# Second norm's weight and bias applied in the second feed-forward's input stage, via DRAM; last norm's as fused VectorE operations

## The chip, the cores and the metric

The kernel runs on one core of a Trainium2 chip. The metric is the device time of one execution in microseconds. The engines are TensorE (PE, matmuls), VectorE (DVE), ScalarE (ACT), GpSimd (POOL) and SyncE (SP), which issues most of the DMAs. Each engine works through its own instructions in a fixed order and waits for the others on semaphores.

## The reference

One layer of an encoder on 1024 tokens of 1024 features in float32, in three sub-layers with a residual and a norm each. The change touches the second norm and the third sub-layer:

```
h  = x * (1 + scale) + shift                    # modulation, from the vector c
y  = (silu(h @ w_in[:, :2816]) * (h @ w_in[:, 2816:])) @ w_out
x  = layer_norm(ALPHA * x + 0.5 * (1 + gate) * y) * g + b
```

The mixer before it ends in the same way, with ln2_g and ln2_b. The third sub-layer uses the mixer's normed result twice: in h, and in the residual ALPHA * x. The output is the third sub-layer's x, with ln3_g and ln3_b.

## The kernel before, in words

All products are done as three float32r products of a high and a low part: `split` has ACT write the high part (L139, a cast) and DVE the low part (L140, a tensor_tensor). The tile names end in h and l, or the halves of one tile are the two parts (gl, wr).

The second feed-forward has two stages. The input stage, `in_phase`, goes through 22 steps j; a step is a pair of column tiles of w_in, whose seven Strassen-Winograd products PE makes (L378). The weights of step j + 1 are loaded and prepared during step j: `in_load` loads them into the tiles "ra" and "rb", two buffers each, on SP (L340); `in_gate` and `in_sums` make the operands "ah", "al", "sh", "sl" (L355 to L358 are the sums on DVE). The results go to DRAM tiles gd (L399). After each step from 2 on a hook is called; in the second feed-forward, `hook2` computes the gate row gate2 at steps 10 to 15, from loads of w_ada (L162) through heap slots. The heap has 30 slots of 4 KB per partition; the right operands of the stage take 28.

The output stage, `out_phase`, multiplies what lies in gd by w_out, in seven products numbered 2, 1, 3, 6, 5, 7, 4, each over 11 steps, four token tiles and three matmuls (L589). `prep` loads gd and w_out four steps ahead (L556, L549) and splits them; at products 1, 5 and 6 DVE also makes sums of the weights (L570, L571, L581, L583). When a product ends, its four PSUM banks are read (L608 to L632), times the gate row (L599), and added to ALPHA * x (L596). `xs2` brings x: the mixer's normed rows before weight and bias, which `done2` stored in the DRAM tiles spill2 (L1257). It loads a row tile (L1417) and has POOL multiply by ln2_g (L266) and add ln2_b (L267), both 128x1024, in `affine`. The rows of weight and bias are loaded into SBUF once, as a broadcast to all partitions (L262).

`done3` is the last norm of a tile. Tiles 0 to 3 are finished after product 5, between the steps of product 7; tiles 4 to 7 after product 4, the last, in which the tiles' matmuls end one after the other. For tiles 0 to 6 `norm_tile` makes the statistics (L247, L249), the reciprocal root in ten small steps (L213 to L223), a factor nm (L256), and has ACT scale (L257); then POOL applies ln3_g and ln3_b to each half (L266, L267), and SP stores it (L1432). Tile 7 takes another way: DVE subtracts the mean and multiplies by ln3_g in one operation of 1024 columns (L1437), multiplies by the reciprocal root and adds ln3_b in one for each half (L1440), and SP and ACT store one half each.

Each engine's order is made ahead of time by a planner from estimated durations and the place in the program; instructions whose inputs the planner expects early are drawn ahead of their place. Buffers with one tag are handed out in turn, and a tile's load waits until the last reader of the buffer's former tile is done.

The first feed-forward uses the same `in_phase` and `out_phase`. There x comes from the input without weight and bias, and its norm is scaled on ACT alone.

Of the kernel before, what the change touches and what calls it, by code (L numbers as in the profile page):

```python
# [7 lines left out]
F32 = mybir.dt.float32  # L8
# [7 lines left out]
P = 128  # L16
# [34 lines left out]
def layer_kernel(ctx, tc, a, out):  # L51
# [26 lines left out]

# [1 line left out]
    c_raw = const.tile([P, KD], F32, name="c_raw")  # L80
# [61 lines left out]

# [1 line left out]
    w_ada = a["w_ada"][0].rearrange("(p j) n -> p j n", j=KD)  # L144
# [64 lines left out]

# [1 line left out]
    def rstd_of(var, eps, name):  # L211
# [56 lines left out]

# [1 line left out]
    def transpose4(name, srcs):  # L270
# [7 lines left out]

    # Strassen-Winograd right operands of a pair of feature tiles (2 k, 2 k + 1); token halves are the columns.
    def right_first(name, ops, hb, eng=V):  # L280
        """hb: feature tiles 2 k and 2 k + 1 of token half 0."""
        hi, lo = slot(f"{name}bh"), slot(f"{name}bl")
        split(hi, lo, hb, eng)
        ops["B11"].append((hi[:, 0], lo[:, 0]))
        ops["B21"].append((hi[:, 1], lo[:, 1]))

    def right_second(name, ops, hb, hc, eng=G, lo=V):
        """hc: feature tiles 2 k and 2 k + 1 of token half 1."""
        t12 = slot(f"{name}t12", dt=F32)
        eng.tensor_tensor(t12[:, 0], hc[:, 0], hb[:, 0], ALU.subtract)  # L290
        eng.tensor_tensor(t12[:, 1], hc[:, 1], t12[:, 0], ALU.subtract)
        right_t(name, ops, 1, t12, lo)
        return t12
# [23 lines left out]

# [1 line left out]
    TAGS = {  # L319
# [4 lines left out]
    def in_tags(wp, order):  # L324
        """Has the tiles that are free first lie first."""
        for tag in order.split():
            shape, bufs = TAGS[tag]
            wp.tile(shape, F32, tag=tag, bufs=bufs, name=f"{tag}_")
# [43 lines left out]
    def product(ps, left, right, ks=range(4), more=False):  # L372
        """more: on top of the sum that the bank holds."""
        wh, wl = left
# [17 lines left out]
    def in_steps(wp, s, j, L, ops, gd, begun={}):  # L392
        """The seven products of a pair of gate and up tiles; the left operands of the second half to DRAM."""
        q = G if j >= NJ - 1 else SY
# [10 lines left out]
        def prod(left, right, ps=None):  # L405
            """ps: the bank that holds the sum so far."""
            if left in begun:
                return begun[left]
            more = ps is not None
            ps = ps if more else bank(f"fi{s}_{j}{left}")  # L410
            product(ps, L[left], ops[right], more=more)
            return ps
# [120 lines left out]

    # ---- SwiGLU, second half: product with w_out in Strassen-Winograd form (token halves, halves of the columns,
    # even and odd feature tiles), residual; done(t) follows each finished token tile; after(half, k) the tiles
    # of a half, some way into the next products ----
    def out_phase(s, wp, w_out, gd, gate, xs, done, after, hook):
# [13 lines left out]
        def prep(n, k):  # L551
            """Operands of step k of product n; wa holds B11, then T1, and B22, wb B12, then T3, and B21, then T4."""
            if (n, k) in left:
# [137 lines left out]

    # ================= sub-layer 1 =================
    x_in = a["x"][0]
    with pool("p1a") as wp:
# [27 lines left out]
        def first_mod(kk, raws, n):  # L722
            """The last n of its four blocks are summed on the vector engine first."""
            ps = wide(f"ada0p{kk}")
# [46 lines left out]
        def early(wp, s, w_in, ops):  # L771
# [9 lines left out]

            # a: ada loads, x: token loads, w: weights, M: modulation, H: modulated features, R: right
            # operands, G and S: left operands, g: products; "d" has the vector engine take more of it
            for tok in SEQ.split():
# [49 lines left out]
    rows = tc.alloc_tile_pool(name="rows", bufs=1, reuse_waits="tile", side="right")  # L834
    gate1 = rows.tile([P, D], F32, name="gate1")
    mix_in = a["mix_w_in"][0]
# [59 lines left out]

    # ================= sub-layer 2 =================
    mxb = tc.alloc_tile_pool(name="mxb", bufs=1, reuse_waits="tile", side="right")
# [191 lines left out]
    with pool("mattn") as wp:  # L1090
# [64 lines left out]

        # LayerNorm over the channels of the convolution, in place, between the steps of the attention
        cstat = {}
# [78 lines left out]

    spill2 = [dram.tile([P, D], F32, name=f"spill2_{t}", tag="spill2", bufs=NT) for t in range(NT)]
    ops = new_ops()
    hb, hc = [None] * 4, [None] * 4
    todo2 = {}  # L1240
    TENG = (V, G)
    with pool("p3a") as wp:
# [59 lines left out]
        def play(st, tokens):  # L1302
            """m: output projection, d: residual norm, f and F: features of the token halves, r: B11 and B21,
            b: B22, s, t: sums and parts of T1 and T2, u, v: of T3 and T4, G: A11, A12 and A22, X, x: sums and
            parts of S1 and S2, Y, y: of S3 and S4, p: products, W: the next weights; a capital letter at the
            end is the engine, "!" keeps the order on the engine."""
            n3 = {t[-2]: t[-1] for t in reversed(tokens) if t.lstrip("!")[0] == "p" and t[-1] in "35"}
# [77 lines left out]
        play(None, first)  # L1385

        def hook2(j):
            if j in (10, 13):
                if j == 10:
                    mods["gate2"] = slot("gate2", (P, D), F32)  # L1390
                todo2[j + 2] = ada_gate(wp, raw_slot, 2, 0.5, mods["gate2"], (j - 10) // 3)
            if j in todo2:
                todo2.pop(j)()
# [9 lines left out]
    raw_pool[2].release()  # L1403
    rows.release()

    with pool("p3b") as wp:
        xt2 = {}
        got2 = set()
        rows2 = []
        fin = []  # L1410

        def xs2(t):
            if t not in got2:
                got2.add(t)
                if t not in xt2:
                    xt2[t] = wp.tile([P, D], F32, tag="x", bufs=XB, name=f"x2_{t}")
                SY.dma_start(xt2[t], spill2[t])  # L1417
                if not rows2:
                    rows2.extend((row_bcast("ln2_g", wp), row_bcast("ln2_b", wp)))
                affine(xt2[t], *rows2)  # L1420
            return xt2[t]

        def done3(t):
            if not fin:
                fin.extend((row_bcast("ln3_g"), row_bcast("ln3_b")))
            rows_ = out[t * P : (t + 1) * P, :]
            if t < NT - 1:
                norm_tile(xt2[t], f"3_{t}")
                for h in range(2):
                    hs = slice(h * H, (h + 1) * H)  # L1430
                    affine(xt2[t][:, hs], fin[0][:, hs], fin[1][:, hs])
                    SY.dma_start(rows_[:, hs], xt2[t][:, hs])  # L1432
                return
            x = xt2[t]
# [7 lines left out]

        out_phase(2, wp, a["ffn2_w_out"][0], gd, mods["gate2"], xs2, done3, lambda half, k: None, lambda gi, j: None)


# [35 lines left out]
```

## Time and profile before

| | us |
|---|---|
| three runs | 1960.56, 1960.99, 1962.79 |
| median | 1960.99 |
| profiled execution, first to last instruction (span) | 1958.3 |
| PE busy | 1832.7 (94%) |
| DVE busy | 1538.3 (79%) |
| ACT busy | 781.3 (40%) |
| POOL busy | 405.6 (21%) |

The profiled execution's own time is taken as its span and what lies around it. The page cuts the span into 40 slices of 49 us; a digit is a busy share in tenths, PEclk the clock granted to TensorE in tenths of full speed:

```profile
PE   5899999999999999999999859989999999997896
DVE  8867768675697978999689989896565756589888
POOL 2200000000000020168476561430000000036034
PEclk7899999999999999999999879989999999998998
```

The second feed-forward's input stage fills slices 27 to 34, its output stage the last five. Busy times of PE are from modelled ends; a matmul of 512 columns is shown with 0.39 us and the next one starts earlier.

### The profile page before, as it was taken

Reading aid. Unit: us, or ns where it says so; the run is one execution under the profiler, and the core shown is the slowest. Engines: PE = TensorE matmul, PEld = TensorE weight load, DVE = VectorE, ACT = ScalarE, POOL = GpSimd, SP = SyncE. Lnnn points to the kernel's source line nnn. Section 1 sums busy time; section 2 is a strip of 40 time slices with the busy share of each in tenths; the row PEclk is TensorE's granted clock in tenths of the full one; section 3 lists DMA queues with packets and bytes.
Section 4 is the critical chain, followed back from the end, with each engine's and each line's share of the span. In section 5 each row is a group of like instructions: output and inputs, shape, how many; then the busy total and the mean of one; then the engine's idle time right before and its main releaser. Section 6 shows DMA issues by size and latency. Waiting matters only on the chain. (4 is left out here: it accounts for less than half of the span.)

```text
span 1958.3 us, 23453 instructions
## 1 busy us (share of the span) xinstructions
PE 1832.7 (94%) x8562; PEld 1514.4 (77%) x8562; DVE 1538.3 (79%) x2276; ACT 781.3 (40%) x1240; POOL 405.6 (21%) x280
## 2 busy tenths in 40 slices
PE   5899999999999999999999859989999999997896
PEld 4688888888888788888888748768888888885675
DVE  8867768675697978999689989896565756589888
ACT  3423333333445441142677642643333333443541
POOL 2200000000000020168476561430000000036034
PEclk7899999999999999999999879989999999998998
DMA  8527445533885322110000032234333432574511
GB/s 251 166 92 223 157 140 188 167 119 130 302 282 155 113 95 62 33 44 33 1 1 1 25 124 78 97 114 139 102 100 116 129 97 86 192 261 155 162 65 70
DMA packets 201394, 238.39 MB, mean 122 GB/s; under 512 B 13866, under 2 KB 124575, under 8 KB 201278
## 3 DMA queue, kind: packets, MB, share of 16 engines
q1 hardware_dynamic: 197786, 225.06, 35.7%
q0 software_dynamic: 2112, 7.34, 1.0%
q10 hardware_dynamic: 1380, 4.49, 0.6%
q8 instruction: 67, 1.10, 0.2%
q14 instruction: 49, 0.40, 0.1%
HBM read 183.89 MB, written 52.95 MB: 121 GB/s over the span
## 5 line engine op out<-in xcount | busy, mean ns | idle before, releaser
L589 PE MATMUL fo<-wr,gl 128*128 128x512 f32 x1848 | 430.4, 394 | 25.8 <-DVE wr L140 13.3
L589 PEld LDWEIGHTS fo<-wr,gl 128*128 128x128 f32 x1848 | 349.2, 190 | 105.0 <-DVE wr L140 16.0
L140 DVE TENSOR_TENSOR sl<-sf,sh 128x1024 fp32r<-128x1024 f32 x87 | 110.6, 1272 | 145.2 <-ACT sh L139 145.2
L139 ACT CAST sh<-sf 128x1024 fp32r<-128x1024 f32 x88 | 92.7, 1053 | 209.9 <-issue 31.5
L399 POOL DMA_DIRECT2D gd<-gf x8 | 4.5, 568 | 824.9 <-DVE gf L465 824.3
L932 DVE SCALAR_TENSOR_TENSOR cacc<-u,convw,cacc 128x1015 f32<-128x1015 f32 (+14 forms) x120 | 152.3, 1319 | 0.9
L140 DVE TENSOR_TENSOR gl<-gr,gl 128x512 fp32r<-128x512 f32 x148 | 110.6, 754 | 8.1 <-ACT gl L139 6.7
L139 ACT CAST gl<-gr 128x512 fp32r<-128x512 f32 x148 | 90.6, 618 | 64.1 <-DMA gr<-gd 56.2
L153 DVE SCALAR_TENSOR_TENSOR ada<-adaw,c_act,ada 128x512 f32<-128x512 f32 x98 | 73.3, 748 | 36.5 <-DMA adaw<-in_w_ada_dram 35.7
L266 POOL TENSOR_TENSOR x<-x,row_ln_g 128x1024 f32<-128x1024 f32 (+1 forms) x28 | 65.0, 2334 | 169.1 <-ACT x L257 100.8
L1058 DVE TENSOR_REDUCE mx<-sc 128x1 f32<-128x1024 f32 x64 | 76.1, 1216 | 19.8 <-PE sc L1056 19.8
L1060 ACT ACTIVATE p<-sc,mx 128x1024 f32<-128x1024 f32 x64 | 71.3, 1115 | 48.0 <-DVE mx L1058 46.7
L139 ACT CAST ah<-ra 128x1536 fp32r<-128x1536 f32 x44 | 65.0, 1478 | 58.6 <-DMA ra<-in_ffn_w_in_dram 14.4
L140 DVE TENSOR_TENSOR al<-ra,ah 128x1536 fp32r<-128x1536 f32 x44 | 77.1, 1751 | 1.2 <-ACT ah L139 1.2
L427 ACT ACTIVATE gf<-gf 128x512 f32<-128x512 f32 x44 | 27.8, 632 | 118.5 <-DVE gf L426 109.7
L140 DVE TENSOR_TENSOR wr<-wa,wr 128x512 fp32r<-128x512 f32 x66 | 54.1, 819 | 23.7 <-ACT wr L139 23.6
L1293 PE MATMUL mo<-moh,fh 128*128 128x512 f32 x128 | 51.3, 401 | 20.7 <-DVE x L1297 20.1
L139 ACT CAST wr<-wa 128x512 fp32r<-128x512 f32 x66 | 41.1, 622 | 62.4 <-PE fo L589 61.8
L913 PE MATMUL glu<-hm,gluh 128*128 128x512 f32 x256 | 65.7, 392 | 0.0
L1112 POOL TENSOR_TENSOR p<-p,p 128x1024 f32<-128x1024 f32 x27 | 64.8, 2401 | 1.9
L1129 PE MATMUL av<-vf,aT 128*128 128x128 f32 x512 | 62.7, 276 | 1.2 <-ACT cacc L1190 0.8
L139 ACT CAST wr<-wb 128x512 fp32r<-128x512 f32 x66 | 40.1, 620 | 55.3 <-PE fo L589 45.3
(3503 smaller groups left out, 4858.8 us busy)
## 6 DMA issues: line engine op xcount, KB each, us to landing
gr<-gd SPq DMA_DIRECT2D x148, 256.0 KB, 3.0
ra<-in_ffn_w_in_dram SPq DMA_DIRECT2D x132, 256.0 KB, 4.1
adaw<-in_w_ada_dram SPq DMA_DIRECT2D x56, 512.0 KB, 4.0
gd<-gf SPq DMA_DIRECT2D x102, 256.0 KB, 2.1
rb<-in_ffn_w_in_dram SPq DMA_DIRECT2D x44, 256.0 KB, 3.1
wb<-in_ffn_w_out_dram SPq DMA_DIRECT2D x44, 256.0 KB, 5.0
wa<-in_ffn_w_out_dram SPq DMA_DIRECT2D x44, 256.0 KB, 4.8
gd<-s SPq DMA_DIRECT2D x40, 256.0 KB, 4.2
```

The costliest lines, as they stand in the source:

```text
L139: a = S.copy(hi, x)
L140: b = eng.tensor_tensor(lo, x, hi.bitcast(F32), ALU.subtract)
L153: V.scalar_tensor_tensor(acc, raw[:, jj], c_act[:, n : n + 1], acc, ALU.mult, ALU.add)
L266: eng.tensor_tensor(x, x, g, ALU.mult)
L589: PE.matmul(ps, lhsT=g[:, x, ts_], rhs=w[:, y], start=n in (1, 2, 3) and k == i == 0, stop=k == NK - 1 and i == 2, skip_group_check=n not ...
L913: PE.matmul(q[2 * m + h], lhsT=w[:, m * P : (m + 1) * P], rhs=hm[k][h][:, x], start=k == 0 and n == 0, stop=k == KD - 1 and n == 2,)
L932: V.scalar_tensor_tensor(acc[:, lo_t:hi_t], u[:, lo_t + sh : hi_t + sh], convw[:, i, jj : jj + 1], acc[:, lo_t:hi_t], ALU.mult, ALU.add,)
L1058: V.tensor_reduce(mx_, ps, axis=AX.X, op=ALU.max, negate=True)
L1060: S.activation(pe, ps, AF.Exp, bias=mx_, accum_out=sm[:, e : e + 1])
L1112: last = G.tensor_tensor(p0, p0, p1, ALU.add)
L1129: PE.matmul(ps[:, 0:P], lhsT=aT[:, kt], rhs=vf[kt][:, h * P : (h + 1) * P], start=kt == 0, stop=kt == 7)
L1293: pe = PE.matmul(ps, lhsT=x[:, ts_], rhs=w[:, ds_], start=n == 0, stop=n == total - 1)
```

## The change

The second norm's weight and bias are applied earlier, and the result goes through DRAM once more. In steps 2 to 9 of the second feed-forward's input stage, `hook2` calls `residual_tile`: it loads a row tile of spill2 on SP into a buffer of the tag "ra" (shared with the weight tiles of `in_load`), has DVE multiply by ln2_g and add ln2_b, and stores it on SP into new DRAM tiles spill3. The two rows ln2_g and ln2_b take heap slots from step 2 to step 9. `xs2` then loads from spill3, and POOL does nothing there. gate2 lies where gate1 lay (the pool rows, released later), and not in a heap slot. `done3` treats tiles 0 to 6 as tile 7 was treated: one fused DVE operation of 1024 columns and two of 512, and one store from SP and one from ACT.

```diff
     rows = tc.alloc_tile_pool(name="rows", bufs=1, reuse_waits="tile", side="right")
-    gate1 = rows.tile([P, D], F32, name="gate1")
+    gate1 = rows.tile([P, D], F32, tag="gate1", name="gate1")
...
+        rows2 = []
+
+        def residual_tile(t):
+            if t == 0:
+                rows2.extend((row_bcast("ln2_g"), row_bcast("ln2_b")))
+            x = raw_pool[2].tile([P, 3, 4, P], F32, tag="ra", bufs=2, name=f"x2a_{t}")
+            x = x.rearrange("p a b c -> p (a b c)")[:, 0:D]
+            SY.dma_start(x, spill2[t])
+            affine(x, *rows2, V)
+            SY.dma_start(spill3[t], x)
+            if t == NT - 1:
+                rows2.clear()
+
         def hook2(j):
+            if j < NT + 2:
+                residual_tile(j - 2)
             if j in (10, 13):
                 if j == 10:
-                    mods["gate2"] = slot("gate2", (P, D), F32)
+                    mods["gate2"] = rows.tile([P, D], F32, tag="gate1", name="gate2")
...
-                SY.dma_start(xt2[t], spill2[t])
-                if not rows2:
-                    rows2.extend((row_bcast("ln2_g", wp), row_bcast("ln2_b", wp)))
-                affine(xt2[t], *rows2)
+                SY.dma_start(xt2[t], spill3[t])
             return xt2[t]
...
         def done3(t):
             if not fin:
                 fin.extend((row_bcast("ln3_g"), row_bcast("ln3_b")))
             rows_ = out[t * P : (t + 1) * P, :]
-            if t < NT - 1:
-                norm_tile(xt2[t], f"3_{t}")
-                for h in range(2):
-                    hs = slice(h * H, (h + 1) * H)
-                    affine(xt2[t][:, hs], fin[0][:, hs], fin[1][:, hs])
-                    SY.dma_start(rows_[:, hs], xt2[t][:, hs])
-                return
             x = xt2[t]
             mv = tile_stats(x, f"3_{t}")
             r = rstd_of(mv[:, 1:2], EPS, f"3_{t}")
             V.scalar_tensor_tensor(x, x, mv[:, 0:1], fin[0], ALU.subtract, ALU.mult)
             for h in range(2):
                 hs = slice(h * H, (h + 1) * H)
                 V.scalar_tensor_tensor(x[:, hs], x[:, hs], r, fin[1][:, hs], ALU.mult, ALU.add)
                 (SY, S)[h].dma_start(rows_[:, hs], x[:, hs])
```

## Rows read from the trace of the kernel before

**Rows 1.** Windows: stretch, length, busy us (instructions) by engine, granted clock, DMA share, GB/s.
```profile
1775.00:1800.00 25.00, 12.82 (x39) 9.38 (x38) 25.00 (x18) 4.03 (x7) 17.68 (x7) 0.74 0.40 127
1800.00:1850.00 50.00, 41.29 (x172) 32.99 (x171) 45.48 (x68) 26.34 (x48) 11.19 (x2) 0.93 0.43 129
```
**Rows 2.** Windows of equal length in the first and the second output stage.
```profile
490.50:699.00 208.50, 208.43 (x920) 170.50 (x920) 178.15 (x324) 100.81 (x171) 7.87 (x11) 1.00 0.61 203
1701.40:1909.90 208.50, 182.75 (x774) 148.12 (x774) 185.66 (x267) 92.04 (x156) 71.38 (x31) 0.95 0.51 174
```
**Rows 3.** PE's groups, first and second output stage; then a wait in the second.
```profile
L589 PE MATMUL fo<-wr,gl 128*128 128x512 f32 x924 | 212.8, 391 | 0.1
...
L589 PE MATMUL fo<-wr,gl 128*128 128x512 f32 x924 | 217.5, 397 | 25.8 <-DVE wr L140 13.3 <-ACT pu L608 7.6 <-DVE pv L632 4.9
...
ACT gl L139 <- DMA gr<-gd: 51.0, 22, 9.8
```
**Rows 4.** Timeline of PE: start, length, what, how many in the row.
```profile
1500.73 0.39 PE L378 MATMUL fi_11A<-r_0t3h,ah 128*128 128x512 f32 x1
...
1503.45 0.39 PE L378 MATMUL fi_12A<-r_0bh,ah 128*128 128x512 f32 x1
...
1696.70 9.68 PE L589 MATMUL fo<-wr,gl 128*128 128x512 f32 x42
...
1909.47 30.54 PE L589 MATMUL fo<-wr,gl 128*128 128x512 f32 x132 [1.70 <-DVE pv L632]
```
**Rows 5.** Timeline of POOL in the second output stage.
```profile
1741.78 2.67 POOL L266 TENSOR_TENSOR x<-x,row_ln_g 128x1024 f32<-128x1024 f32 x1 [40.02 <-DMA row_ln_g<-in_ln_g_dram]
...
1810.54 2.72 POOL L267 TENSOR_TENSOR x<-x,row_ln_b 128x1024 f32<-128x1024 f32 x1
```
**Rows 6.** Timeline of DVE at that time.
```profile
1742.10 2.90 DVE L571 TENSOR_TENSOR wb<-wb,t 128x512 f32<-128x512 f32 x1
...
1758.97 0.68 DVE L571 TENSOR_TENSOR wb<-wb,t 128x512 f32<-128x512 f32 x1
```
**Rows 7.** Timeline of DVE in the last four tiles.
```profile
1925.76 0.69 DVE L599 TENSOR_TENSOR ev<-fo,gate 128x512 f32<-128x512 f32 x1 [1.64 <-PE fo L589]
...
1927.21 1.29 DVE L247 BATCH_NORM_STATS2 st<-x 128x6 f32<-128x512 f32 x2
...
1930.53 0.16 DVE L221 SCALAR_TENSOR_TENSOR rz<-rt,rz 128x1 f32<-128x1 f32 x1
1930.72 0.15 DVE L223 TENSOR_SCALAR rr<-rz 128x1 f32<-128x1 f32 x1
1930.79 0.68 DVE L599 TENSOR_TENSOR ev<-fo,gate 128x512 f32<-128x512 f32 x1
...
1945.40 0.68 DVE L599 TENSOR_TENSOR ev<-fo,gate 128x512 f32<-128x512 f32 x1
...
1947.89 2.01 DVE L1437 SCALAR_TENSOR_TENSOR x<-x,mv,row_ln_g 128x1024 f32<-128x1024 f32 x1
...
1952.60 0.87 DVE L221 SCALAR_TENSOR_TENSOR rz<-rt,rz 128x1 f32<-128x1 f32 x1
...
1953.69 1.42 DVE L1440 SCALAR_TENSOR_TENSOR x<-x,rr,row_ln_b 128x512 f32<-128x512 f32 x2
```
**Rows 8.** Timeline of DVE, then of SP, around one weight tile of the input stage.
```profile
1351.27 0.69 DVE L355 TENSOR_TENSOR sf<-rb,ra 128x512 f32<-128x512 f32 x1
...
1368.57 1.23 DVE L140 TENSOR_TENSOR sl<-sf,sh 128x1024 fp32r<-128x1024 f32 x1 [0.22 <-ACT sh L139]
...
1372.12 1.75 DVE L140 TENSOR_TENSOR al<-ra,ah 128x1536 fp32r<-128x1536 f32 x1
...
1373.90 1.47 SPq L340 DMA_DIRECT2D ra<-in_ffn_w_in_dram  x3
```
**Rows 9.** Windows: one step of the input stage.
```profile
1351.40:1370.40 19.00, 19.00 (x85) 15.73 (x84) 12.16 (x17) 6.36 (x9) 0.00 (x0) 1.00 0.41 139
```
**Rows 10.** DMA issues: KB each, median us from issue to landing.
```profile
ra<-in_ffn_w_in_dram SPq DMA_DIRECT2D x132, 256.0 KB, 4.1
```

More of the change, by code (lines that the diff above doesn't have):

```diff
@@ L1237, in layer_kernel @@
     spill2 = [dram.tile([P, D], F32, name=f"spill2_{t}", tag="spill2", bufs=NT) for t in range(NT)]
+    spill3 = [dram.tile([P, D], F32, name=f"spill3_{t}", tag="spill3", bufs=NT) for t in range(NT)]
     ops = new_ops()
@@ L1403, in layer_kernel @@
     raw_pool[2].release()
-    rows.release()
     with pool("p3b") as wp:
@@ L1408, in layer_kernel @@
         got2 = set()
-        rows2 = []
         fin = []
@@ L1443, in layer_kernel @@
         out_phase(2, wp, a["ffn2_w_out"][0], gd, mods["gate2"], xs2, done3, lambda half, k: None, lambda gi, j: None)
+    rows.release()
 _INS = [
```

## The prediction

> **What bounds the kernel now.** The page comes first: TensorE (PE) is busy for 94% of the span and VectorE (DVE) for 79%, and the slices of the page's second part put most of the missing 6% of PE at the beginning, once in the middle, and in the last fifth. [...]
>
> This is the second feed-forward's product with w_out. Its twin, the same function for the first feed-forward, is the best control there is: in 208.5 us of it PE is busy for 208.4, although DVE is busy for 178 [rows 2]. In an equal stretch of the second one PE has 182.8. The groups of PE's instructions name who is late: the 924 matmuls of the phase have 0.1 us of idle time before them in the twin and 25.8 here, 13.3 for DVE's low parts of the weights, 7.6 for an ACT copy and 4.9 for the sums on pv [rows 3].
>
> What does the second have and the first not? POOL. In the second, POOL multiplies by ln2_g and adds ln2_b, sixteen operations, the first and the last in [rows 5]. Just there a 128x512 tensor_tensor of DVE takes 2.90 us, and 0.68 us as soon as POOL rests [rows 6]; six in a row are that long. POOL and DVE stand in each other's way, so some 40 us of POOL work, which nobody seems to wait for, is what makes DVE late.
>
> The size of the loss: PE's first matmul of the phase starts at 1696.70 us, the last run of them ends at 1909.47 + 30.54 = 1940.01 [rows 4], 243.3 us. That the 924 matmuls are 7 products x 11 steps x 4 tiles x 3 stands in the code; twelve take 1503.45 - 1500.73 = 2.72 us at the full clock [rows 4], so 0.2267 us each and 209.5 us in all. The loss is 33.8 us: 25.8 of waiting and 8.0 that the lower clock after the waits costs. Behind PE stands a tail of 1958.3 - 1940.0 = 18.3 us, in which DVE is hardly ever idle.
>
> **The change part by part.** The profiled execution's span is 1958.3 us; the median of the runs is 1960.99, so 2.7 us lie around it, and they stay.
>
> (a) The sixteen POOL operations leave the phase, and the two row loads with them. With POOL silent DVE does as in the twin, and PE needs 209.5 us: -33.8. Bounds: 0 if POOL were not the cause, -33.8 at best, since nothing below 209.5 can be had. I take the whole, because the twin loses 0.1 us with the same products, the same buffers but two and the same DVE work [rows 2].
>
> (b) In the first seven tiles of the last norm, nm on DVE, the scaling on ACT and four POOL operations become one DVE operation of 1024 columns and two of 512. At 1024 columns DVE takes 1.23 us for two inputs from SBUF [rows 8]; the pair of 512 took 1.42 [rows 7]; 2.6 us a tile. Tiles 0 to 3 fall into product 7, where DVE must read pv in time or PE can't begin product 4. That is 10.6 us more DVE work, against the POOL work that disturbs it there now. The wait is 4.9 us now [rows 3]; the twin, which in the same product sums 8 blocks for a gate, has none. Bounds 0 and 4.9 + 2.8, the latter because ACT now issues the second store of each tile and holds the casts queued behind it until DVE's last half (0.7 us, four tiles). I take 1.0, near the twin.
>
> (c) The tail. DVE's last four tiles begin at 1925.76 and end at 1953.69 + 1.42 = 1955.11, 29.35 us [rows 7]. PE's last four groups, of 7 steps x 3 matmuls, end 21 x 0.2267 = 4.8 us apart and are faster than that: DVE sets the end. Tile 4 takes 1930.79 - 1925.76 = 5.0 us undisturbed. Tile 7 takes 1955.11 - 1945.40 = 9.7 and has the fused form already, but its 1024-wide operation takes 2.01 instead of 1.23, and three of the one-column L221 steps are stretched, at 0.87 against 0.16 in the worst: together 2.6 us, so 7.1 undisturbed. The other three have one more 0.6 us of statistics (two took 1.29): 3 x 7.7 + 7.1 = 30.2. So +0.9. What the disturbance gives back the fused work takes. Bounds +0.9 and -2.7: a step that needs the one before it starts 0.19 us later (1930.53 to 1930.72), a step of another tile 0.07 later (1930.72 to 1930.79) [rows 7], and three chains of ten such steps between another tile's operations would save up to 3.6. I take +0.9, since today's order hardly mixes the tiles. [...]
>
> (d) In the input stage DVE gets sixteen 128x1024 operations at 1.23 us, 19.7 us, two to a step from step 2 to 9. A step lasts 19 us, and DVE works 12.2 of them in the fuller kind [rows 9], so 2.5 us fit into 6.8 idle ones. Bounds: 0 (PE has no gap here to gain) and 19.7 if every one delays PE. I take 1.0 for the whole stage: an operation that stands in DVE's order before its 512 KB have landed holds the reads of PSUM behind it, and PE's next product into that bank waits for those.
>
> (e) SP gets eight loads, eight stores and two row loads there, each issue under 0.5 us, and each store holds SP until DVE has added the bias; behind it stand the next weights and the gd stores. The cover is that a weight tile is issued a step ahead. But the loaded row tile takes one of the two "ra" buffers in turn with the weights, so that these are single-buffered for eight steps. Now: DVE first reads a weight tile at 1351.27, last at 1372.12 + 1.75 = 1373.87, and the load into that buffer is issued at 1373.90 [rows 8] and lands 4.1 us after issue, three in a row: some 5.6 us [rows 10]. With one buffer this tile's load would start when the tile before it was read, a step earlier, at 1354.8, and end by 1360.4. What its sums feed is needed by DVE at 1368.57 [rows 8], and two sums of 0.7 us and a cast of ACT of about 1 us come before that: some 5 us are to spare. Cost 0; without that cover see the second rival.
>
> (f) gate2 leaves the heap for the place of gate1. Its two rounds of loads and sums lose their free heap slots to the two rows and come later than now, into the same idle DVE time; it is needed at the start of the phase some 200 us on. 0.
>
> Sum: -33.8 + 1.0 + 0.9 + 1.0 = -30.9; span 1927.4, with the 2.7 us around it **1930 us**.
>
> **The rivals.**
> *Loads, not DVE, set products 6 and 5.* The 7.6 us wait for the ACT copy came when DVE had caught up, and ACT's casts stood behind loads of gr, 51.0 us in all [rows 3]. If it stays with its share of the slow clock (some 2.4) and product 7's wait grows to the 7.7 of (b), the time is 1930 + 10 + 6.7 = 1947. For: the fused work comes in the same products. Against: the twin moves 203 GB/s where this one moves 174 [rows 2], without a wait.
> *Slower: the single weight buffer decides.* If DVE's first read keeps its place in the order, a tile's cycle is 22.6 us of reading and 5.6 of loading, 28.2 against 19.04 a step: +9.2 us in each of eight steps, 73 in all, 2003 us. It decides from 30.9 / 8 = 3.9 us a step on. For: the sums are read early today. Against: they are read early because nothing holds them, and 5 us are to spare.
> *The added DVE work is exposed.* 18.7 more than I took in (d): 1949 us. Against: 6.8 idle us a step.
> *POOL is not the cause, and the moved work changes nothing:* 1961. The stretch from 0.68 to 2.90 us in step with POOL speaks against it.
>
> **How the numbers follow.** Forecast 0.68, loads and product 7 0.13, exposed DVE work 0.08, single buffer 0.08, no change 0.03. The forecast's own range goes from 1924.6 (no losses in (b) and (d), the tail at -2.7) to 1938, with the small terms at several times my value. With the first rival it reaches 1947 and holds four in five: 1924 to 1947. Under 0.2%, some 4 us, a measurement of this kernel tells nothing from no change: faster 0.89, same 0.03, slower 0.08.
>
> **What would show it.** After: no POOL operation but the gate's copy in the phase; no 128x512 operation of DVE over 1 us; PE's phase at 210 to 212 us from first to last matmul with a clock of 1.0 (a); no wait of PE for DVE's wr (a), under 2 us for pv (b); 29 to 30 us from the first ev of the tail to DVE's end (c); steps of 19.0 us in the input stage while the row tiles pass (d, e). Steps of 20 us or more there, or PE waiting for ah or sh, would make the prediction wrong, and so would a wait for the ACT copy of pu that stays.

## The result and the profile after

The changed kernel takes 1924.64 us (median of 1924.09, 1924.61, 1924.68 and 1927.3) against 1961.14 us of the kernel before on the same chip: a ratio of 0.9821, 95% interval 0.9807 to 0.9834. The prediction of 1930 us had the direction and the place; 5.4 us of the gain of 36.5 were not forecast, and the result lies at the lower end of the forecast's own range (1924.6 to 1938). The profiled run of the changed kernel is the slowest of the four, with a span of 1925.5 us.

First the windows that answer to [rows 1]; the columns are the same.

```profile
1775.00:1800.00 25.00, 25.00 (x112) 20.71 (x111) 24.67 (x40) 12.64 (x23) 0.00 (x0) 1.00 0.34 103
1800.00:1850.00 50.00, 50.00 (x221) 41.15 (x220) 33.14 (x52) 29.44 (x51) 0.00 (x0) 1.00 0.51 161
```

PE (first) works without a gap at the full clock (1.00). DVE (third) does 40 operations in the first window where it did 18, in the same busy time, and in the second it rests for 16.9 us. POOL (fifth) is silent.

PE's group of the output stage, and its timeline, answer to the second row of [rows 3] and the last of [rows 4]:

```profile
L589 PE MATMUL fo<-wr,gl 128*128 128x512 f32 x924 | 210.2, 389 | 0.1
```
```profile
1700.65 210.31 PE L589 MATMUL fo<-wr,gl 128*128 128x512 f32 x924
```

All 924 products stand in one row, since nothing waits: 210.3 us where it was 243.3. The waits for wr, pu and pv are gone.

DVE in the first 19 us of what was POOL's stretch (1741 to 1760), by groups: count, busy us, mean ns of one. [rows 6] had 2.90 us there.

```profile
L140 DVE TENSOR_TENSOR gl<-gr,gl 128x512 fp32r<-128x512 f32 x8 | 5.5, 684 | 0.0
L583 DVE TENSOR_TENSOR wb<-wa,wb 128x512 f32<-128x512 f32 x8 | 5.4, 684 | 0.0
```

The tail answers to [rows 7]. These are the first and last rows of DVE there, the `ev` of each tile, and at the second tile a few small steps beside it.

```profile
1897.39 0.69 DVE L599 TENSOR_TENSOR ev<-fo,gate 128x512 f32<-128x512 f32 x1 [0.28 <-PE fo L589]
1898.12 0.69 DVE L596 SCALAR_TENSOR_TENSOR x<-x,ev 128x512 f32<-128x512 f32 x1
1898.85 1.29 DVE L247 BATCH_NORM_STATS2 st<-x 128x6 f32<-128x512 f32 x2
...
1900.35 1.27 DVE L1442 SCALAR_TENSOR_TENSOR x<-x,mv,row_ln_g 128x1024 f32<-128x1024 f32 x1
1901.54 0.15 DVE L216 TENSOR_SCALAR rz<-rv 128x1 int32<-128x1 int32 x1
1901.60 0.68 DVE L599 TENSOR_TENSOR ev<-fo,gate 128x512 f32<-128x512 f32 x1
1902.20 0.14 DVE L217 TENSOR_SCALAR rz<-rz 128x1 int32<-128x1 int32 x1
...
1906.29 0.68 DVE L599 TENSOR_TENSOR ev<-fo,gate 128x512 f32<-128x512 f32 x1
...
1912.27 0.68 DVE L599 TENSOR_TENSOR ev<-fo,gate 128x512 f32<-128x512 f32 x1
...
1920.95 1.42 DVE L1445 SCALAR_TENSOR_TENSOR x<-x,rr,row_ln_b 128x512 f32<-128x512 f32 x2
```

From the first `ev` to DVE's end it is 1922.37 - 1897.39 = 25.0 us, 29.4 before. Tile 5's `ev` (1901.60) stands between two steps of tile 4's square root (L216 and L217): the work of two tiles is mixed. In the kernel before, tile 4's small steps run to the last one, L223 at 1930.72, ahead of tile 5's `ev` at 1930.79 [rows 7], and one small operation of tile 4 (nm) stands behind it:

```profile
1931.39 0.21 DVE L256 TENSOR_SCALAR nm<-mv,rr 128x1 f32<-128x1 f32 x1
```

The input stage grew. DVE's two operations on the row tiles, with what ended the idle time before them, then one of the two steps where PE lost time (step 8; step 9 follows):

```profile
L266 DVE TENSOR_TENSOR x2a<-x2a,row_ln_g 128x1024 f32<-128x1024 f32 x8 | 9.8, 1223 | 10.7 <-DMA x2a<-spill 9.1 <-DMA gd<-gf 1.7
L267 DVE TENSOR_TENSOR x2a<-x2a,row_ln_b 128x1024 f32<-128x1024 f32 x8 | 9.8, 1223 | 0.2
```
```profile
1440.11 1.23 DVE L266 TENSOR_TENSOR x2a<-x2a,row_ln_g 128x1024 f32<-128x1024 f32 x1 [1.61 <-DMA x2a<-spill]
...
1444.89 0.49 DVE L151 TENSOR_SCALAR ada<-adaw,c_act 128x512 f32<-128x512 f32 x1 [1.17 <-DMA adaw<-in_w_ada_dram]
1445.30 0.68 DVE L357 TENSOR_TENSOR sf<-ra,rb 128x512 f32<-128x512 f32 x1
1445.90 0.68 DVE L443 TENSOR_TENSOR p<-fi_8A,p 128x512 f32<-128x512 f32 x1
...
1462.27 1.54 DVE L153 SCALAR_TENSOR_TENSOR ada<-adaw,c_act,ada 128x512 f32<-128x512 f32 x2 [2.72 <-DMA adaw<-in_w_ada_dram]
```
```profile
1446.63 0.50 PE L378 MATMUL fi_8A<-r_0t3h,ah 128*128 128x512 f32 x1 [0.52 <-DVE p L443]
```

In step 8 DVE waits for a load of the row tile, then for one of the gate's columns (adaw), and the sum on `p`, which frees PE's bank, stands behind both. In step 9 it stands behind the gate's columns alone (2.72 us). From the start of its first product to that of the next step's, step 8 lasts 19.90 us and step 9 20.25, where steps 4 to 7, and the same two in the kernel before, last 19.04. The gate's first sum is at 1444.89 us here; it was at 1307.44 in the kernel before and is at 1306.82 in the run without the residual tiles ("No detour" below), so the tiles and their two rows push the gate's loads back into steps 8 and 9. From the first product of the input stage to the first of the output stage it is 1700.65 - 1257.12 = 443.5 us, 441.8 before. This is one run; the second profile of the same kernel (below) has 442.9.

The span in four stretches, both profiled runs, each end taken from PE's timeline:

| stretch | before | after | difference |
|---|---|---|---|
| start to first product of the second input stage | 1254.9 | 1257.1 | +2.2 |
| input stage | 441.8 | 443.5 | +1.8 |
| output stage, PE | 243.3 | 210.3 | -33.0 |
| end of PE to the end | 18.3 | 14.6 | -3.7 |
| span | 1958.3 | 1925.5 | -32.8 |

The same code runs in the first row's stretch. The ten profiled runs that have the residual tiles began their input stage at 1254.8 to 1261.0 us (1257.0 on the mean), the four that have not at 1254.3 to 1256.5 (1255.2). These ranges overlap; whether the change has a part in the 2.2 us is not shown.

### The profile page after: what moved, and what is told of

Same layout as the page of the kernel before. It is cut to its first block, busy times and chain, and to the rows that moved or that the text cites. A ratio compares the mean times of both kernels' runs of the same rounds, so it can differ in the third digit from the quotient of the medians.

```text
span 1925.5 us, 23435 instructions
## 1 busy us (share of the span) xinstructions
PE 1829.6 (95%) x8562; PEld 1512.7 (79%) x8562; DVE 1518.1 (79%) x2306; ACT 773.0 (40%) x1233; POOL 321.0 (17%) x236
## 4 chain that ended last, share of the span: by engine, by line
PE 70%; DVE 16%; issue 8%; DMA 3%; ACT 2%; POOL 1%; SPq 1%; DVEq 0%; POOLq 0%; ACTq 0%
PE fo L589 19%; PE mo L1294 4%; PE vp L961 2%; DVE mx L1058 2%; PE qp L961 2%; PE fi_16A L378 1%; PE fi_15A L378 1%; PE fi_10A L378 1%; PE fi_6A L378 1%; PE fi_2A L378 1%; PE fi_21A L378 1%; PE fi_19A L378 1%; PE fi_20A L378 1%; PE fi_18A L378 1%; PE fi_17A L378 1%
## 5 line engine op out<-in xcount | busy, mean ns | idle before, releaser
L589 PE MATMUL fo<-wr,gl 128*128 128x512 f32 x1848 | 423.1, 390 | 0.2
L140 DVE TENSOR_TENSOR sl<-sf,sh 128x1024 fp32r<-128x1024 f32 x87 | 109.4, 1259 | 116.0 <-ACT sh L139 115.8
L140 DVE TENSOR_TENSOR gl<-gr,gl 128x512 fp32r<-128x512 f32 x148 | 102.1, 696 | 6.9 <-ACT gl L139 5.5
L140 DVE TENSOR_TENSOR al<-ra,ah 128x1536 fp32r<-128x1536 f32 x44 | 77.0, 1750 | 1.3 <-ACT ah L139 1.2
L427 ACT ACTIVATE gf<-gf 128x512 f32<-128x512 f32 x44 | 27.8, 632 | 124.1 <-DVE gf L426 113.7
L140 DVE TENSOR_TENSOR wr<-wa,wr 128x512 fp32r<-128x512 f32 x66 | 45.5, 689 | 27.4 <-ACT wr L139 27.2
L1129 PEld LDWEIGHTS av<-vf,aT 128*128 128x128 f32 x512 | 60.9, 195 | 1.7 <-ACT cacc L1190 1.0
```

The costliest lines, as they stand in the source:

```text
L140: b = eng.tensor_tensor(lo, x, hi.bitcast(F32), ALU.subtract)
L589: PE.matmul(ps, lhsT=g[:, x, ts_], rhs=w[:, y], start=n in (1, 2, 3) and k == i == 0, stop=k == NK - 1 and i == 2, skip_group_check=n not ...
L1129: PE.matmul(ps[:, 0:P], lhsT=aT[:, kt], rhs=vf[kt][:, h * P : (h + 1) * P], start=kt == 0, stop=kt == 7)
```

## The experiments

The theory: VectorE is held up by GpSimd when both work on whole tiles, and this alone makes PE wait. The rivals: the loads, the dependences of the residual, or the order of VectorE's work.

| kernel | median us | ratio to before, 95% | input stage | PE in output stage | behind PE |
|---|---|---|---|---|---|
| part one alone | 1935.05 | 0.9859 (0.9841 to 0.9877) | 441.3 | 215.5 | 18.2 |
| part two alone | 1951.44 | 0.9950 (0.9935 to 0.9964) | 440.9 | 238.7 | 14.6 |
| GpSimd beside, two inputs | 1952.85 | 0.9953 (0.9939 to 0.9968) | 441.5 | 237.4 | 14.6 |
| GpSimd beside, one input | 1943.94 | 0.9919 (0.9903 to 0.9936) | 441.1 | 229.4 | 14.6 |
| GpSimd beside, fills | 1925.39 | 0.9817 (0.9802 to 0.9833) | 441.9 | 210.3 | 14.8 |
| no detour | 1923.28 | 0.9807 (0.9793 to 0.9822) | 441.1 | 210.3 | 15.1 |
| VectorE in the output stage | 1925.27 | 0.9823 (0.9809 to 0.9838) | 440.7 | 210.3 | 15.3 |
| tail in turn | 1928.33 | 0.9836 (0.9821 to 0.9850) | 442.1 | 210.3 | 19.4 |
| nine steps apart | 1925.24 | 0.9821 (0.9806 to 0.9835) | 441.4 | 210.3 | 14.1 |
| ScalarE's statistics | 1925.19 | 0.9820 (0.9806 to 0.9834) | 442.7 | 210.9 | 15.3 |
| the same, nine steps apart | 1923.85 | 0.9816 (0.9802 to 0.9830) | 441.1 | 211.1 | 13.6 |
| the changed kernel again | 1923.07 | 0.9813 (0.9799 to 0.9827) | 442.9 | 210.3 | 14.6 |

The last three columns are us of each profiled run, worked out as in the table above. Each ratio is to the kernel before in runs beside it, whose medians were 1959.6 to 1962.0 us. Line numbers in the rows of an experiment are those of its own kernel: where an edit adds lines, L599 can become L601 or L602, and L596 become L599.

**Part one alone, and part two alone.** The first restores the old branch of `done3`, the second is the kernel before without that branch.

```diff
             rows_ = out[t * P : (t + 1) * P, :]
+            if t < NT - 1:
+                norm_tile(xt2[t], f"3_{t}")
+                for h in range(2):
+                    hs = slice(h * H, (h + 1) * H)
+                    affine(xt2[t][:, hs], fin[0][:, hs], fin[1][:, hs])
+                    SY.dma_start(rows_[:, hs], xt2[t][:, hs])
+                return
```

> The changed kernel with the second part undone: token tiles 0 to 6 are normed and then multiplied and added in halves on GpSimd again, the residual stays as changed. Theory (GpSimd beside VectorE in the output stage makes VectorE slow, each part carries its own price): the loss beside the first eight residual tiles is gone, but the wait of the products on the operands in the last product (4.9 us before) and the 29.4 us of the last four tiles come back, so the time is 1924.6 + about 9 = 1934 us (1930 to 1937), a ratio to the kernel before near 0.986. Rival 1 (the second part frees most of the time): 1944 or more. Rival 2 (the tail's gain comes from the first part too): 1926 or less.

> The kernel before with the second part alone: the last norm's weight and bias fused into two VectorE operations for every tile, the residual still on GpSimd in the output stage. Theory: 4.9 us of waits in the last product and 4 us of tail go, the 20.9 us of waits beside the residual tiles stay: 1961.1 - 9 = 1952 us (1949 to 1956). The gains of this run and of the run with the first part alone add up to the whole change's 36.5 us within 4 us. Rival (the fused operations put four times as long an operation into VectorE's order and it has no room): 1961 or more.

PE's group of the output stage in the first, then in the second:

```profile
L589 PE MATMUL fo<-wr,gl 128*128 128x512 f32 x924 | 212.0, 391 | 3.5 <-DVE pv L632 3.5
```
```profile
L589 PE MATMUL fo<-wr,gl 128*128 128x512 f32 x924 | 218.3, 399 | 20.4 <-DVE wr L140 12.3 <-ACT pu L608 7.9
```

With part one alone only the wait for pv stays, in product 7, where GpSimd still works on the last norm. With part two alone the waits for wr and pu stay, beside the residual tiles. The gains are 26.9 and 10.5 us, 37.4 together, and 36.5 were measured for both: the parts add up. Part one brings 27.8 of the 33.0 us in PE's stretch, part two the other 5.2 (4.6 where it is alone) and all of the 3.7 behind PE (18.2 stays with part one alone, 14.6 is there with part two alone).

**GpSimd beside the output stage.** The changed kernel, with one of three kinds of GpSimd work that no result needs. Two inputs:

```diff
                 SY.dma_start(xt2[t], spill3[t])
+                junk = wp.tile([P, D], F32, tag="junk", bufs=1, name=f"junk_{t}")
+                G.tensor_tensor(junk, xt2[t], mods["gate2"], ALU.mult)
+                G.tensor_tensor(junk, xt2[t], mods["gate2"], ALU.add)
```

> The changed kernel, with GpSimd made busy again in the output stage: for each residual tile two of its 128x1024 operations with two inputs read the tile just loaded and the gate row and write into a tile that nobody reads. VectorE and TensorE have the same work as in the changed kernel; one thing is tied to it, that the tile is written by the residual only when GpSimd has read it. Theory (VectorE loses its speed beside GpSimd's two-input operations): the loss of the kernel before comes back, VectorE's 128x512 operations beside GpSimd's take 2 to 3 us instead of 0.68, the product row group waits 18 to 22 us, the time is 1924.6 + 20 to 28 = about 1949 us (1943 to 1955). Rival (it was the loads, the rows of weight and bias, or the dependence of the residual on GpSimd's result): 1925 to 1929 us.

PE's group, then GpSimd and VectorE side by side:

```profile
L589 PE MATMUL fo<-wr,gl 128*128 128x512 f32 x924 | 219.3, 400 | 18.1 <-DVE wr L140 13.5 <-ACT pu L608 4.6
```
```profile
1772.00 2.41 POOL L1434 TENSOR_TENSOR junk<-x,gate 128x1024 f32<-128x1024 f32 x1 [12.05 <-DMA x<-spill]
1774.49 2.69 POOL L1435 TENSOR_TENSOR junk<-x,gate 128x1024 f32<-128x1024 f32 x1
1778.11 2.47 POOL L1434 TENSOR_TENSOR junk<-x,gate 128x1024 f32<-128x1024 f32 x1 [0.94 <-DMA x<-spill]
```
```profile
1771.86 1.28 DVE L615 TENSOR_TENSOR pu<-fo,pu 128x512 f32<-128x512 f32 x2
1773.06 1.90 DVE L599 TENSOR_TENSOR pu<-pu,gate 128x512 f32<-128x512 f32 x1
1774.88 2.84 DVE L140 TENSOR_TENSOR wr<-wa,wr 128x512 fp32r<-128x512 f32 x1
1777.65 0.68 DVE L596 SCALAR_TENSOR_TENSOR x<-x,pu 128x512 f32<-128x512 f32 x1
1778.25 2.88 DVE L599 TENSOR_TENSOR pu<-pu,gate 128x512 f32<-128x512 f32 x1
```

The loss returns: PE needs 237.4 us, and waits for the same two things as with part two alone. The rows show how. GpSimd's first operation ends at 1772.00 + 2.41 = 1774.41, and VectorE's L599 beside it 0.55 us later; GpSimd's second ends at 1777.18, VectorE's L140 0.54 later; the third at 1780.58, L599 0.55 later. An undisturbed operation follows the one before after 0.60 (1901.60 to 1902.20 in the changed kernel's tail). So the rows read as if VectorE did not run slowly beside GpSimd, but stood still until GpSimd's operation is over and then did its own at full speed. In the gap before 1778.11, where GpSimd waits for a load, the L596 takes 0.68. And the two L615 at 1771.86, of which one input lies in PSUM (`fo`), take 1.28 together although GpSimd started at 1772.00: they are not held. The dependence that the edit brings along (a tile may be overwritten only when GpSimd has read it) is not the cause: in this run and in the next no wait of VectorE in the stage is put down to GpSimd.

One input:

```diff
+                junk = wp.tile([P, D], F32, tag="junk", bufs=1, name=f"junk_{t}")
+                for _ in range(4):
+                    G.tensor_scalar(junk, xt2[t], 1.0, 0.0, ALU.mult, ALU.add)
```

> The changed kernel, with GpSimd busy in the output stage by operations with one input: for each residual tile four 128x1024 multiply-adds by constants read the tile just loaded and write into a tile that nobody reads, 32 in all. The one such operation that both kernels have (the copy of the gate row, 1.14 us at 1704.56 after) lies beside three VectorE operations that take 2.73 us instead of 1.9. Theory (any GpSimd operation on whole tiles holds VectorE up, about 0.7 us for each us): 32 x 1.14 = 36 us of GpSimd work, some 25 us taken from VectorE, which has some 10 us of idle time there, so the time is 1924.6 + 10 to 20 = about 1940 us (1934 to 1948). Rival (only operations with two inputs do it): 1925 to 1929 us, and VectorE's 128x512 operations stay at 0.68.

PE's group, GpSimd's, and VectorE beside it:

```profile
L589 PE MATMUL fo<-wr,gl 128*128 128x512 f32 x924 | 216.1, 396 | 13.3 <-DVE wr L140 7.3 <-ACT pu L608 5.9
```
```profile
L1435 POOL TENSOR_SCALAR junk<-x 128x1024 f32<-128x1024 f32 x32 | 46.2, 1443 | 49.1 <-issue 37.8 <-DMA x<-spill 8.9
```
```profile
1774.13 1.53 DVE L140 TENSOR_TENSOR wr<-wa,wr 128x512 fp32r<-128x512 f32 x1
1775.58 1.53 DVE L596 SCALAR_TENSOR_TENSOR x<-x,pu 128x512 f32<-128x512 f32 x1
1777.04 0.68 DVE L615 TENSOR_TENSOR pu<-fo,pu 128x512 f32<-128x512 f32 x1
1777.64 0.93 DVE L140 TENSOR_TENSOR gl<-gr,gl 128x512 fp32r<-128x512 f32 x1
```

One input is enough: the median is 19 us above the changed kernel's. One operation of each engine alternates, 1.45 us from one VectorE start to the next (1774.13 to 1775.58), and again L615 with its PSUM input takes 0.68. It goes the other way too: one of GpSimd's operations lasts from 1767.56 to 1772.22, 4.66 us, and VectorE's beside it stay at 0.67 to 0.68. There it is GpSimd that is held: 4.66 us against 1.44 on the mean.

Fills:

```diff
+                G.tensor_scalar(junk[:, 0:1], xt2[t][:, 0:1], 1.0, 0.0, ALU.mult, ALU.add)
+                for _ in range(4):
+                    G.memset(junk, 0.0)
```

> The changed kernel, with GpSimd busy in the output stage by fills alone: for each residual tile, once it is loaded (a one-column operation waits for it), four fills with zero of a 128x1024 tile that nobody reads. GpSimd reads nothing but the one column. Theory A (any GpSimd operation on whole tiles holds VectorE, reading or not): VectorE's 128x512 operations beside the fills go up from 0.68 to about 1.5 us as beside the one-input operations, the time is 1935 to 1945 us. Theory B (GpSimd's reads hold VectorE, or the fills use a path of their own): 0.68 stays, 1924 to 1927 us. I hold A for the likelier, 6 in 10.

GpSimd's fills, PE's group, and a group of VectorE from 1745 to 1790 us, in the midst of the fills:

```profile
L1436 POOL MEMSET junk<- 128x1024 f32 x32 | 30.6, 957 | 1.9
```
```profile
L589 PE MATMUL fo<-wr,gl 128*128 128x512 f32 x924 | 210.2, 389 | 0.1
```
```profile
L140 DVE TENSOR_TENSOR gl<-gr,gl 128x512 fp32r<-128x512 f32 x17 | 11.6, 685 | 0.0
```

My likelier theory was wrong: 30.6 us of fills cost nothing, and VectorE's operations stay at 0.69. The operations of GpSimd that hold VectorE read SBUF, the fills don't. That the fills are free for another reason (the second half of theory B) is not ruled out by a run of its own. But GpSimd's only reads here, the eight one-column operations ahead of the fills, take 0.19 to 3.68 us each, so they seem to be held by VectorE, while a fill takes 0.96 on the mean. The three kernels agree with the reading as the cause: 2.88 and 1.53 us against readers, 0.68 with an input in PSUM, 0.69 against fills. How one engine holds the other was not shown.

**No detour.** The changed kernel without `residual_tile`; the second norm's weight and bias are left out of the residual.

```diff
-            if j < NT + 2:
-                residual_tile(j - 2)
...
-                SY.dma_start(xt2[t], spill3[t])
+                SY.dma_start(xt2[t], spill2[t])
```

> The changed kernel without the residual tiles in the input stage: the output stage loads the normed tile without the second norm's weight and bias, which are left out of the residual. The rest is as it is. Theory (the 16 VectorE operations and 24 transfers cost the input stage what its steps show, about 1.8 us): 1924.6 - 1.8 = 1922.8 us (1921.5 to 1924.2). Rival 1 (they are hidden wholly, and what the steps show is from run to run): 1924.6 within 0.7. Rival 2 (they cost 4 us or more, also where mixer steps came 2.2 us later): 1920.6 or less.

1923.28 us is where the first theory has it, but the changed kernel's second measurement is 1923.07, so the medians don't tell 1.8 us from nothing. The profiles tell more: the input stage is 441.9 us on the mean over the ten profiled runs that have the residual tiles (441.1 to 443.5) and 441.1 over the four that have not (440.7 to 441.8). The detour costs 0.8 us on the mean there, and single runs with it lie from nothing to 2.4 above the mean of the others. The losses of its two dearest runs lie in steps 8 and 9, where the loads come late; that the landing of loads sets the price in every run was not tested.

**VectorE in the output stage.** The kernel before with part two, and with the residual's weight and bias on VectorE where GpSimd did them.

```diff
-                affine(xt2[t], *rows2)
+                affine(xt2[t], *rows2, V)
```

> The kernel before with the second part, and with the residual's weight and bias on VectorE in the output stage: no detour through the second DRAM copy, GpSimd silent as in the changed kernel. Theory (VectorE has no room there: 16 operations of 1.22 us, 19.7 us, against 4.3 us idle from 1775 to 1800, 8.9 us from 1800 to 1850 and about 1 us from 1750 to 1775 in the changed kernel): the input stage is 0 to 2 us shorter, TensorE waits 4 to 8 us in the output stage, together 1924.6 + 4 = 1928.6 us (1926 to 1933). Rival (the order has room, the detour buys nothing): 1922 to 1925 us.

```profile
1775.00:1800.00 25.00, 25.00 (x112) 20.72 (x111) 24.91 (x42) 13.20 (x24) 0.00 (x0) 1.00 0.39 119
1800.00:1850.00 50.00, 50.00 (x222) 41.15 (x221) 46.95 (x72) 28.85 (x52) 0.00 (x0) 1.00 0.52 160
```

My theory failed, and by a reading error: for VectorE's idle time I had taken a wrong column, PEld's. In the changed kernel's windows VectorE has 0.3 and 16.9 us to spare, not 4.3 and 8.9, and most of the 19.4 us of added work went into the 16.9 (33.1 to 47.0 busy). PE waits nowhere, and 1925.27 us is the changed kernel's time. So the transfers through DRAM and the move into the input stage buy nothing; that GpSimd leaves the stage does.

**The tail, one tile behind the other.**

```diff
-                y = wp.tile([P, H], F32, tag="tmp", bufs=2, name=f"ev{s}{t}")
-                gated(y, ps, lower)
-                residual(4 + t, lower, y)
-                done(4 + t)
+                with tc.issue_after(in_turn[-1]) if in_turn else nullcontext():
+                    y = wp.tile([P, H], F32, tag="tmp", bufs=2, name=f"ev{s}{t}")
+                    gated(y, ps, lower)
+                    residual(4 + t, lower, y)
+                    done(4 + t)
...
+                if t > 3:
+                    in_turn[:] = [last.ins]
```

> The changed kernel, with VectorE's work on the last four tiles put strictly one tile behind the other: no operation of a tile is issued before the last one of the tile ahead. The same operations, GpSimd silent. Theory (the tail is shorter than forecast since the operations of two tiles fill each other's waits): the four tiles take 30.2 us as in the prediction instead of 25.0, so the time is 1924.6 + 5.2 = 1929.8 us (1928 to 1931). Rival (the order is of no weight, a silent GpSimd is what makes the tail short): 1924 to 1926 us.

```profile
1893.64 0.69 DVE L601 TENSOR_TENSOR ev<-fo,gate 128x512 f32<-128x512 f32 x1 [0.29 <-PE fo L591]
...
1897.51 0.15 DVE L218 TENSOR_SCALAR rz<-rz 128x1 int32<-128x1 int32 x1
1897.70 0.27 DVE L221 TENSOR_SCALAR rt<-rz,rv 128x1 f32<-128x1 f32 x1
...
1922.02 1.42 DVE L1448 SCALAR_TENSOR_TENSOR x<-x,rr,row_ln_b 128x512 f32<-128x512 f32 x2
```

1923.44 - 1893.64 = 29.8 us: the forecast's 30.2 is what the tail takes in turn. 0.19 us lie between the starts of two dependent steps (1897.51 to 1897.70), where 0.06 lie between L216 and the next tile's L599 in the changed kernel. The stretch from PE's first product of the output stage to the end is 229.7 us against 224.9, so the mixing is worth 4.8 us; the medians differ by 3.7 and 5.3 from the two of the changed kernel.

**Three attempts at a shorter tail.** `STAGGER` 9 instead of 7 in the second output stage; the sums and sums of squares of tiles 0 to 6 on ScalarE; both.

```diff
-            cut = NK - {7: TM, 4: STAGGER}.get(n, 1)
+            cut = NK - {7: TM, 4: STAGGER + 2 * (s == 2)}.get(n, 1)
```
```diff
-            mv = tile_stats(x, f"3_{t}")
+            for h in range(2):
+                S.activation(sq, x[:, h * H : (h + 1) * H], AF.Square, accum_out=acc[:, 2 + h : 3 + h])
+                S.activation(sq, x[:, h * H : (h + 1) * H], AF.Copy, accum_out=acc[:, h : h + 1])
...
```

> The changed kernel with the last product's tiles finished nine steps apart instead of seven (27 multiplications, 6.1 us, instead of 21 and 4.8 us), in the second output stage alone: three of the four last tiles reach VectorE 2.7, 1.4 and 0 us nearer to its own 5.7 us per tile, and the first one 4.1 us earlier. Theory A (VectorE sets the tail, and its operand work for the last steps, which ends at 1896.4, gives way): 1924.6 - 2 to 4 = about 1921.5 us. Theory B (the operands of the last two steps come too late for the first tile, so TensorE waits for them what the tail saves): 1924 to 1928 us. I hold B for a little likelier, since VectorE was busy without a gap from 1879.8 to 1897.1 in the changed kernel.

> The changed kernel, with the statistics of the last norm's tiles 0 to 6 taken by ScalarE (sums and sums of squares beside its copies) and put together by three one-column operations on VectorE; tile 7 as it is. Theory (VectorE sets the tail, 25.0 us for four tiles that PE finishes 4.8 us apart, and ScalarE has 3 of 25 us to do there): VectorE loses about 1.1 us a tile, the last tile then begins when PE ends instead of 1.3 us later and its chain is not mixed with that of tile 6: 1924.6 - 2.5 = 1922 us (1920.5 to 1924). Rival 1 (the chain of small steps sets the tail, not VectorE's busy time): 1924.6 within 1. Rival 2 (ScalarE's sums stand in the way of its casts of the operands, so PE waits in the last product): 1926 or more.

> The run with ScalarE's statistics, and nine steps between the last tiles instead of seven in the second output stage. Theory (nine steps bought 0.4 us alone because VectorE was still in arrears from product 7 when the first tile was done; with about 8 us taken from it the tiles 4 to 6 are over when PE ends): what is left behind PE is the chain of one tile, 7.1 us, a store of 3.1 and the start, so 1924.6 - 3.5 = 1921 us (1919.5 to 1923). Rival (the arrears stay, or the operands come late): as the run with seven steps, 1922 or more.

With nine steps PE waits no more than before, so theory B's mechanism is not there, but theory A's gain isn't either. VectorE's order, around the first tile's `ev`:

```profile
1890.68 1.28 DVE L599 TENSOR_TENSOR pv<-pv,gate 128x512 f32<-128x512 f32 x2
1891.88 1.29 DVE L596 SCALAR_TENSOR_TENSOR x<-x,pv 128x512 f32<-128x512 f32 x2
1893.09 0.68 DVE L599 TENSOR_TENSOR ev<-fo,gate 128x512 f32<-128x512 f32 x1
```

The upper halves of two tiles, which the changed kernel does before its tail, now stand behind the operands and directly before the first `ev`, which has no idle time before it: most of the work has only changed places, and the stretch from PE's first product to the end is 224.4 us instead of 224.9. ScalarE's statistics take VectorE's 1.3 us a tile away and bring a wait in their place:

```profile
1895.24 0.69 DVE L599 SCALAR_TENSOR_TENSOR x<-x,ev 128x512 f32<-128x512 f32 x1
1898.30 0.21 DVE L1451 TENSOR_SCALAR mv<-acc 128x1 f32<-128x1 f32 x1 [2.36 <-ACT sq L1447]
```

Four passes of 0.63 us and four readings of the sum of 0.19 follow one another on ScalarE, and VectorE, which needed 1.3 us, waits for 2.36. What is saved in work is lost in the chain. None of the three differs from the changed kernel by more than its measurement is uncertain; no version that beats it was found.

**The changed kernel again.**

> The changed kernel itself once more, beside the others of this group. Theory (the profiled run of the changed kernel was a late one: its mixer began 1.6 to 2.2 us later with the same code, and in the input stage a late load of the gate's columns cost 1.8 us): a median of 1923 to 1926 us; in the trace the input stage, from its first product to the first product of the output stage, takes 441.8 us (as before) to 443.5 (as in the first profile of the changed kernel); with the loads landing in time 442. The output stage from first product to the end takes 224.9 us, within 0.7. Rival (the residual tiles cost the input stage 1.8 us in every run): 443.5 us again.

The median is 1923.07 us, the input stage 442.9, the rest 224.9 from the first product of the output stage to the end. The rival (1.8 us in every run) is out; the detour's price varies.

## Why the prediction was right, and where not

- *The limit.* Right: PE waited for VectorE, and VectorE for GpSimd. That the twin stage without GpSimd work is the control was the reading that carried the forecast, and the fills show why a count of GpSimd's busy time alone would not have: 30.6 us of fills cost nothing.
- *(a) and (b), -33.8 and +1.0 in PE's stretch.* The sum was -32.8, measured -33.0. The split was not quite so: the whole loss was put down to the sixteen residual operations, and they account for 27.8; 5.2 came from GpSimd's part of the last norm, so the fused operations in product 7 bring a gain where a cost of 1.0 was taken. The two errors, 6.0 and 6.2 us, cancel in the sum, because both terms were taken against one floor of 209.5 us; the stretch takes 210.3 with 0.1 us of idle time.
- *(c) the tail, +0.9.* This step failed, and it is most of the error: behind PE it measured -3.7, and from the first `ev` to DVE's end 25.0 us instead of 30.2. The durations were right (29.8 us in turn), and it is true of today's order that it "hardly mixes the tiles": one small operation of a tile stands behind the next tile's `ev`. What failed is the overlap: today's order was taken for that of the changed kernel, in which the steps of one tile go between those of another, worth 4.8 us. Why it mixes was not tested; in the old form the chains of three tiles go on through ScalarE and GpSimd, in the fused form all steps are VectorE's. Of (c)'s two rows the one of 0.07 us came nearer: 0.06 lie between L216 and the next tile's L599. My bound of -2.7 was too near as well. It counted only the small steps, but a large one gains too: one that needs the one before it starts 0.73 us after it (1898.12 to 1898.85), one of another tile 0.60 after (1901.60 to 1902.20).
- *(d) the input stage, +1.0.* Right in size on the mean (0.8), 1.8 in the first profile. The mechanism is the one named, a VectorE operation waiting for a load ahead of the sum that frees PE's bank; but the load that did most of it is the gate's (adaw), not the row tile's. (f) had the gate's loads come later, at a cost of 0; this 0 failed, since they came where VectorE had no time to wait.
- *(e) the single weight buffer, 0.* Right for PE: steps 4 to 8 of the input stage start 19.04 us apart while the row tiles pass, as before, and what PE waits for most in steps 8 and 9 is the sum on p (0.52 and 0.43 us), not ah or sh. But part of what was to spare is used up: VectorE's first read of a weight tile (L355) waits 8.9 us in seven places for the load, where it was 0.8 in one. Step 9, at 20.25 us, passes the "20 us or more" that was named as a sign against the prediction; it does so for the reason in (d).
- *The rivals.* Loads instead of VectorE: with GpSimd silent the wait for the copy of pu (7.6) is gone, and it comes back with GpSimd alone, 4.6 us with two inputs; so it was a consequence. The slower single buffer did not occur, and exposed VectorE work did not, even where I put all of it into the output stage.
- *The time around the span, 2.7 us.* Mis-sized: it was taken from the median of other runs less the span of the profiled one. Each run of the changed kernel lasts 1.8 us longer than its span (1927.3 against 1925.5).

The forecast of 1930 less the 4.6 us by which (c) was off and the 0.9 around the span is 1924.5; the median is 1924.6. So close a fit is luck in part: the four runs lie between 1924.1 and 1927.3.

## What to carry over

Where GpSimd runs beside a full VectorE, look at the durations of VectorE's operations in the timeline: where those with two SBUF inputs grow and those with a PSUM input don't (2.88 and 0.68 us here), GpSimd's reading is the first suspect, and here its work was cheaper on VectorE itself, in either stage in which it has idle time. The chains of small dependent operations were dearest in turn here (29.8 us for four tiles, 25.0 mixed); put a second chain into the gaps of the first before handing part of it to another engine (ScalarE's part took 1.3 us from VectorE and made it wait 2.36). When a change has two halves, run each alone: here they added up. And where a change takes two steps to one end, leave one out: the detour through DRAM turned out to buy nothing.

## What was not expected of the hardware

- GpSimd's fills of whole tiles (0.96 us for 128x1024) left VectorE's 128x512 operations at 0.69 us, while a one-input operation of GpSimd on a tile of the same size made a 0.68 us operation last 1.53.
- Beside GpSimd's two-input operations a VectorE operation with two SBUF inputs ended 0.54 to 0.55 us after GpSimd's did, in the three pairs shown, as if it waited and then ran at full speed. In the rows shown one operation of each goes in turn, so one of 0.68 us cost 2.88. Where VectorE's went on undisturbed (0.67 to 0.68) it was GpSimd's one-input operation that lasted, 4.66 us against 1.44 on the mean.
